# Layer 0's gate products from q and k: fp32 in four column strips instead of split fp32r one by one

## The chip, the cores and the metric
The kernel runs on one core of one Trainium2 chip, as one program. The metric is the device time of one execution in microseconds; the median of three runs of the kernel before is 917.6 us (916.42 to 917.76). The engines are named as the profile names them: PE is TensorE (PEld its weight loads), DVE is VectorE, ACT is ScalarE, POOL is GpSimd, SP is SyncE, whose queue issues most DMAs.

## What is computed
The reference is a trunk of two layers, an mLSTM mixer (layer 0) and a gated linear attention mixer (layer 1), for one sequence of 512 tokens and a model width of 1024. The part that the change touches is the gates of layer 0. Each of the 512 tokens gets eight gate values, two for each of four heads, from q, k and v, each 2048 wide:

```python
    q = jnp.einsum('bthd,hde->bthe', uch, _f32(wq))
    k = jnp.einsum('bthd,hde->bthe', uch, _f32(wk))
    v = jnp.einsum('bthd,hde->bthe', u.reshape(B, T, M_HEADS, M_HEAD_DIM), _f32(wv))
    gates = (jnp.einsum('bte,eg->btg', q.reshape(B, T, D_INNER), wg[:D_INNER])
             + jnp.einsum('bte,eg->btg', k.reshape(B, T, D_INNER), wg[D_INNER:2 * D_INNER])
             + jnp.einsum('bte,eg->btg', v.reshape(B, T, D_INNER), wg[2 * D_INNER:])
             + _f32(b_gate))
    log_i = gates[..., :M_HEADS]
    log_f = jax.nn.log_sigmoid(gates[..., M_HEADS:])
    hh = mlstm_chunked(q, k * (M_HEAD_DIM ** -0.5), v, log_i, log_f)
```

The gates go through running sums and maxima into exponentials, so they need nearly the full fp32 precision; q, k and v also feed the attention of each head.

## The kernel before
Activations lie with 128 channels on the partitions and the 512 tokens along the free axis, a `t2` tile of 128x512 (59 buffers of that kind). Nearly every product is made as three fp32r matmuls: an operand is split into a rounded part `hi` (an ACT cast) and the rest `lo` (a DVE subtraction), and hi*hi, hi*lo and lo*hi are added in PSUM. PSUM has eight banks, one 128x512 fp32 tile each.

The order of work is written out by hand as a list of jobs. `run_jobs` goes through it: before a job it loads and splits the weight chunks of the next jobs (three raw buffers, chunks split about three jobs ahead), then calls what `later(k, ...)` has put off to this job, then pops from `steps` and `spare`, then issues the job's own matmuls. Each engine runs its queue in the order in which this program issues it; SP's queue holds the loads of weights (`load_raw`, L155), of gate weights for v (L389) and the stores and loads of `uc_d` (L436, L712).

In layer 0, for each head: four `u` jobs (the input projection, then a convolution), two `v` jobs, and four q/k jobs (`qk_job`: two for q, then two for k). A q/k job makes two tiles of q or k with 24 matmuls and splits each into `qkh` and `qkl`. Two jobs later (three for head 0) `gate_add` multiplies each `qkh` and `qkl` with 16 columns of `wgr`, which hold the eight gate weights as `hi` and `lo` parts, into rows 0 to 15 of the bank `gacc`: four fp32r matmuls for a job, 16 jobs. The 64 matmuls and four more with the v part (`v_gates_end`) form one accumulation. The scores of a head (`score`) come after the second `u` job of the next head.

V of a head is copied from PSUM by ACT (`v_evac`), is then read by DVE and POOL for the v part of the gates (`v_gate`, popped from `spare` in later jobs), and stays in its four `t2` tiles until `split_v` of its head, after the gates are done (`decay`, `split_v`). After the last head come the `z` jobs, with `gates1` (copy of `gacc` to `gs`), `gates2` (two fp32 matmuls with the selection matrix `selg` add the hi and lo rows and spread them to 16 rows, then the row operations) and `gates3` between them.

Of the kernel before, what the change touches and what calls it, by code (L numbers as in the profile page):

```python
# [9 lines left out]
F32 = mybir.dt.float32  # L10
# [86 lines left out]
def tile_mlstm_gla(ctx, tc, xT, pvec, cst, wg, wgv, w_min, w_qk, w_v, w_mout,  # L97
# [11 lines left out]
    def t2(name, dt=F32):  # L109
        return tp.tile([P, T], dt, tag="t2", bufs=NT2, name=name)  # L110
# [10 lines left out]
    def mm(out, lhsT, rhs, start, stop, more=False):  # L121

        nc.tensor.matmul(out, lhsT=lhsT, rhs=rhs, start=start, stop=stop, skip_group_check=more)  # L123
# [13 lines left out]
    def split(hi, lo, src):  # L137
        nc.scalar.copy(hi, src)  # L138
        nc.vector.tensor_sub(lo, src, hi.bitcast(F32))  # L139
# [7 lines left out]
    def job(fn, *srcs, n=1, b=0, la=LA):  # L147
        jobs.append((fn, srcs, n, b, la))

    def later(k, fn):  # L150
        laters.append([k, fn])
# [214 lines left out]
    nc.vector.tensor_copy(csr[:, 3 * P:], cs[:, 4 * P:])  # L366

    wgs = t2("wgs")[:, 0:256].rearrange("p (a b) -> p a b", b=8)
    wgr = t2("wgr", F32R).rearrange("p (a b) -> p a b", b=16)
    nc.scalar.dma_start(wgs, wg)  # L370
    hhi, hlo = t2s("hhi", KD, F32R), t2s("hlo", KD, F32R)
    uc_d = dp.tile([KE, P, T], F32, name="uc_d")
    gacc = psum("gacc")
    gcount = [0]

    def gate_add(w, hi, lo):
        for r in (hi, lo):
            mm(gacc[0:16, :], w, r, gcount[0] == 0, False)
            gcount[0] += 1


    vg = cp.tile([P, NH, 4, 8], F32, name="vg")
# [18 lines left out]
    def v_gates(h):  # L401
        for g in (0, 1, 2, 3):
            v_gate_load(h, g)
        spare.extend([lambda g=g, i=i: v_gate(h, g, i) for g in range(8) for i in range(4)])
# [50 lines left out]
    def u_job(n):  # L455
        def run(chunk):
            ps = psum("u")
            if n < 4:
                proj(ps, chunk, ghi, glo)
                fps.append(ps)  # L460
            else:
                proj(ps, chunk, hhi, hlo)
                u_split(n, ps)
                u_conv(n, ps)
            if n == 2:
                acc = None
                for k in range(KD):
                    acc = add_square(acc, xt[k])
                st["accx"] = acc
                nc.scalar.copy(wgr[:, :, 0:8], wgs)  # L470
                nc.vector.tensor_sub(wgr[:, :, 8:16], wgs, wgr[:, :, 0:8].bitcast(F32))
            if n == 3:
                st["rsx"] = rstd_of([st["accx"]], D)
                u_scaled(range(4), fps)
                steps.extend([lambda k=k: h_step((k, k + 1)) for k in range(0, KD, 2)])

        job(run, ring(w_min[n]), b=3, la=1 if n == 2 else LA)

    def v_evac(h, pss):
        V[h] = t2s(f"V{h}", 4)  # L480
        for i in range(4):
            nc.scalar.activation(V[h][i], pss[i], AF.Copy, accum_out=vmean[:, 4 * h + i:4 * h + i + 1])  # L482
        c = vmean[:, 4 * h:4 * h + 4]
        nc.vector.tensor_scalar_mul(c, c, -1.0 / T)
        v_gates(h)

    def v_job(h, c):
        def run(chunk):
            if c == 0:
                st["v"] = [psum("v") for _ in range(4)]  # L490
            pss = st["v"]
            natural(pss, chunk, 2 * c, [uh[4 * h + i] for i in range(4)], [ul[4 * h + i] for i in range(4)], 4)
            if c == 1:
                later(1, lambda: v_evac(h, pss))

        job(run, ring(w_v[2 * h + c]), n=1, b=4)

    def qk_job(h, which, c):
        d = (q, kq)[which]

        def run(chunk):
            whi, wlo = chunk
            for e in range(2):
                n = 4 * h + 2 * c + e
                ps = psum("qk")
                for k in range(4):
                    wh, wl = part(whi, k * 256 + e * P, P), part(wlo, k * 256 + e * P, P)
                    mm(ps, wh, ch[4 * h + k], k == 0, False)
                    mm(ps, wh, cl[4 * h + k], False, False)
                    mm(ps, wl, ch[4 * h + k], False, k == 3)  # L510
                d[n] = t2("qkh", F32R), t2("qkl", F32R)
                split(*d[n], ps)

            def gates():
                for e in range(2):
                    n = 4 * h + 2 * c + e
                    gate_add(wgr[:, 16 * which + n, :], *d[n])

            later(2 if h else 3, gates)

        job(run, ring(w_qk[which, 2 * h + c]), n=1, b=(1, 4, 4, 6)[h])

    def score(h):
        A[h] = t5(f"A{h}")
        for sb in range(4):
            ps = psum("sc")
            ts = slice(sb * P, T)
            sl = slice(sb * P, (sb + 1) * P)
            o = ps[:, 0:WID[sb]]
            for i in range(4):  # L530
                n = 4 * h + i
                mm(o, kq[n][0][:, sl], q[n][0][:, ts], i == 0, False)
                mm(o, kq[n][0][:, sl], q[n][1][:, ts], False, False)
                mm(o, kq[n][1][:, sl], q[n][0][:, ts], False, i == 3)
            nc.scalar.mul(A[h][:, OFF[sb]:OFF[sb] + WID[sb]], o, float(T) ** -0.5)
# [52 lines left out]
    def rows(name):  # L588
        g[name] = t2(name)[0:R16, :]
        return g[name]  # L590

    def gates1():
        v_gates_end()
        nc.vector.memset(br.bitcast(F32), 0.0)
        nc.vector.memset(rows("zr"), 0.0)
        nc.scalar.copy(rows("gs"), gacc[0:16, :])

    def gates2():
        ips, fps = psum("ips"), psum("fps")
        mm(fps[0:R16, :], selg[0:16, 16:32], g["gs"], True, True)  # L600
        mm(ips[0:R16, :], selg[0:16, 0:16], g["gs"], True, True)
        gi, ab, lf = rows("gi"), rows("ab"), rows("lf")
        nc.scalar.activation(ab, fps[0:R16, :], AF.Abs, bias=col(PV_BF, R16))
        nc.vector.tensor_scalar(lf, fps[0:R16, :], scalar1=col(PV_BF, R16), scalar2=0.0,
                                op0=ALU.add, op1=ALU.min)
        use(LNEXP)
        nc.scalar.activation(ab, ab, AF.Exp, scale=-1.0)
        nc.scalar.activation(ab, ab, AF.Ln, bias=1.0)
        nc.scalar.activation(gi, ips[0:R16, :], AF.Identity, bias=col(PV_BI, R16))
        nc.vector.tensor_sub(lf, lf, ab)  # L610
        mrow, fm, gl, ar, bb = (rows(n) for n in ("mrow", "fm", "gl", "ar", "bb"))
        nc.vector.tensor_tensor(fm.rearrange("p (b t) -> p b t", t=P), lf.rearrange("p (b t) -> p b t", t=P),
                                selg[0:R16, 32:36].unsqueeze(2).broadcast_to([R16, 4, P]), op=ALU.mult)
        nc.vector.tensor_tensor_scan(gl, fm, g["zr"], 0.0, op0=ALU.add, op1=ALU.add)
        nc.vector.tensor_sub(ar, gi, gl)
        nc.vector.tensor_tensor_scan(mrow, lf, gi, 0.0, op0=ALU.add, op1=ALU.max)
        nc.vector.tensor_scalar_max(mrow, mrow, 0.0)
        nc.vector.tensor_sub(bb, gl, mrow)
# [15 lines left out]
    def split_scores(h):  # L634
        S[h] = t5("shi", F32R), t5("slo", F32R)
        split(*S[h], A[h])
# [20 lines left out]
    def weigh(h):  # L657
        nc.vector.tensor_mul(A[h], A[h], W[h])
# [86 lines left out]
            split(yhi[n], ylo[n], HC[h][vt])  # L745

    z_job(b=16)
    job(lambda: score(NH - 1))
    job(gates1)
    job(silu_z, n=0)  # L750
    z_job()
    job(silu_z, n=0)
    job(gates2)
    z_job()
    z_job()
# [2 lines left out]
    job(lambda: (decay(0), weigh(0), split_scores(0), split_v(0)))  # L758
    job(lambda: (load_uc(0), load_uc(1)), n=0)
    z_job()  # L760
    job(lambda: (decay(1), steps.extend([lambda: None, lambda: (weigh(1), split_scores(1))])))

    def head_steps(h):
        m_rstd(h)
        if h + 2 < NH:
            decay(h + 2)
        m_y(h, (0, 1))
        if h + 1 == NH:
            m_y(h, (2, 3))
            y_split(h, range(4))  # L770
        else:
            steps.extend([lambda: (split_v(h + 1), m_y(h, (2, 3)), silu_z(), load_uc(4 * h + 4), load_uc(4 * h + 5)),
                          lambda: None,
                          lambda: y_split(h, range(4))])
            if h + 2 < NH:
                steps.append(lambda: (weigh(h + 2), split_scores(h + 2)))
# [637 lines left out]
def _host(inputs):  # L1414
# [16 lines left out]
    for h in range(4):  # L1431
        for sb in range(4):
            j = 4 * h + sb
            for base in (0, 8):
                cst[base + h, 3 * P + j] = 1.0
                cst[base + 4 + h, 3 * P + 16 + j] = 1.0
            cst[j, 3 * P + 32:3 * P + 36] = (np.arange(4) >= sb)
            cst[j, 4 * P + j] = 1.0
            cst[32 + j, 4 * P + j] = 1.0
        cst[64 + 4 * h, 4 * P + 16 + h] = 1.0  # L1440
        cst[96 + 4 * h, 4 * P + 16 + h] = 1.0
# [49 lines left out]
```

## Time and profile before

| | |
|---|---|
| median of the runs | 917.6 us (916.42 to 917.76, 3 runs) |
| profiled execution | 917.5 us, of which the span of the instructions is 915.8 us |
| PE busy | 902.4 us (99%) |
| DVE busy | 630.6 us (69%) |
| ACT busy | 523.3 us (57%) |
| POOL busy | 183.2 us (20%) |
| DMA moved | 147.58 MB, mean 161 GB/s |

The busy time of an engine is the time in which at least one of its instructions was running. Matmuls overlap in their pipeline and their ends are modelled, so the distance between two starts says what one costs, not its duration. The granted clock is the share of TensorE's full clock. An idle engine costs nothing where another one sets the time.

### The profile page before, as it was taken

How to read it: one execution, taken by the hardware profiler on the slowest of the kernel's cores; microseconds unless marked ns; L12 is line 12 of the kernel's file. 1: busy time of each engine (PE TensorE's matmuls, PEld its weight loads, DVE VectorE, ACT ScalarE, POOL GpSimd, SP SyncE). 2: the span in 40 equal slices, each digit the busy share in tenths (PEclk: the TensorE clock that was granted, in tenths of full speed). 3: DMA queues.
4: the chain of work that ended last, by engine and by line, in shares of the span. 5: the costliest groups of instructions: out<-in, count | busy, mean ns of one | idle time of the engine just before them, and what ended most of it. 6: DMA issues, size and time to landing. Idle time of an engine off the chain costs nothing. (4 is left out here: it accounts for less than half of the span.)

```text
span 915.8 us, 12449 instructions
## 1 busy us (share of the span) xinstructions
PE 902.4 (99%) x4624; PEld 760.7 (83%) x4624; DVE 630.6 (69%) x916; ACT 523.3 (57%) x885; POOL 183.2 (20%) x162
## 2 busy tenths in 40 slices
PE   9999999999999999999999999999999999999995
PEld 6887878878877888899999997777888888888874
DVE  5999797886886668788658746743346547478854
ACT  6865685756654558866557626544435345365642
POOL 0022552262250043245002310421000000000121
PEclk9999999999999999999999999999999999999998
DMA  8334344352342223222775694995343736383776
GB/s 309 120 122 147 117 151 137 116 169 97 123 142 69 93 70 115 92 93 69 232 235 198 206 323 166 236 243 140 116 138 114 242 115 200 118 287 104 269 275 138
DMA packets 50882, 147.58 MB, mean 161 GB/s; under 512 B 5792, under 2 KB 10272, under 8 KB 50528
## 3 DMA queue, kind: packets, MB, share of 16 engines
q1 hardware_dynamic: 44832, 120.29, 39.7%
q0 software_dynamic: 5696, 26.22, 10.8%
q8 instruction: 38, 0.62, 0.3%
q14 instruction: 28, 0.23, 0.1%
q10 hardware_dynamic: 288, 0.22, 0.1%
HBM read 129.92 MB, written 34.60 MB: 180 GB/s over the span
## 5 line engine op out<-in xcount | busy, mean ns | idle before, releaser
L139 DVE TENSOR_TENSOR wlo<-raw,whi 128x1024 fp32r<-128x1024 f32 (+1 forms) x146 | 186.3, 1284 | 98.8 <-ACT whi L138 98.1
L138 ACT CAST whi<-raw 128x1024 fp32r<-128x1024 f32 (+1 forms) x146 | 149.9, 1036 | 79.0 <-PE gv L123 24.2
L394 POOL TENSOR_TENSOR vp<-V,wv 128x512 f32<-128x512 f32 x56 | 88.6, 1604 | 177.4 <-ACT V L482 92.6
L123 PE MATMUL op<-yhi,whi 128*128 128x256 f32 x256 | 73.5, 287 | 0.0
L123 PE MATMUL op<-yhi,wlo 128*128 128x256 f32 x256 | 72.5, 283 | 0.4 <-DVE wlo L139 0.4
L123 PE MATMUL op<-ylo,whi 128*128 128x256 f32 x256 | 72.8, 284 | 0.0
L397 DVE SCALAR_TENSOR_TENSOR vp<-V,wv 128x512 f32<-128x512 f32 x72 | 68.0, 987 | 0.0
L163 POOL DMA_DIRECT2D whi<-wpP x8 | 4.3, 536 | 244.7 <-DMA raw<-in_w_gout 216.9
L123 PE MATMUL gz<-g2h,whi 128*128 128x512 f32 x128 | 51.5, 403 | 0.5 <-PEq L1156 0.5
L123 PEld LDWEIGHTS op<-ylo,whi 128*128 128x128 f32 x256 | 49.1, 192 | 1.1 <-DVE ylo L139 0.6
L123 PE MATMUL gz<-g2h,wlo 128*128 128x512 f32 x128 | 49.9, 390 | 0.0
L123 PE MATMUL gz<-g2l,whi 128*128 128x512 f32 x128 | 49.8, 389 | 0.0
L123 PE MATMUL qk<-chi,whi 128*128 128x512 f32 x128 | 49.8, 389 | 0.0
L123 PE MATMUL qk<-chi,wlo 128*128 128x512 f32 x128 | 49.8, 389 | 0.0
L123 PE MATMUL qk<-clo,whi 128*128 128x512 f32 x128 | 49.8, 389 | 0.0
L123 PE MATMUL gv<-whi,g2h 128*128 128x512 f32 x128 | 49.8, 389 | 0.0
L123 PE MATMUL gv<-wlo,g2h 128*128 128x512 f32 x128 | 49.8, 389 | 0.0
L123 PE MATMUL gv<-whi,g2l 128*128 128x512 f32 x128 | 49.8, 389 | 0.0
L123 PEld LDWEIGHTS op<-yhi,wlo 128*128 128x128 f32 x256 | 49.1, 192 | 0.6 <-DVE wlo L139 0.6
L123 PEld LDWEIGHTS op<-yhi,whi 128*128 128x128 f32 x256 | 49.1, 192 | 0.5 <-issue 0.5
L123 PE MATMUL z<-hhi,whi 128*128 128x512 f32 x112 | 44.1, 394 | 0.0
L123 PE MATMUL z<-hlo,whi 128*128 128x512 f32 x112 | 43.7, 390 | 0.0
(286 smaller groups left out, 2503.9 us busy)
## 6 DMA issues: line engine op xcount, KB each, us to landing
raw<-in_w_min SPq DMA_DIRECT2D x30, 512.0 KB, 3.7
raw<-in_w_mout SPq DMA_DIRECT2D x29, 512.0 KB, 4.2
wv<-in_wgv SPq DMA_DIRECT2D x32, 256.0 KB, 3.6
raw<-in_w_qk SPq DMA_DIRECT2D x16, 512.0 KB, 3.7
raw<-in_w_gqk SPq DMA_DIRECT2D x16, 512.0 KB, 4.0
raw<-in_w_gz SPq DMA_DIRECT2D x16, 512.0 KB, 5.2
raw<-in_w_gv SPq DMA_DIRECT2D x16, 512.0 KB, 4.1
raw<-in_w_v SPq DMA_DIRECT2D x8, 512.0 KB, 3.5
```

Source lines behind the costliest of these rows:

```text
L123: nc.tensor.matmul(out, lhsT=lhsT, rhs=rhs, start=start, stop=stop, skip_group_check=more)
L138: nc.scalar.copy(hi, src)
L139: nc.vector.tensor_sub(lo, src, hi.bitcast(F32))
L163: nc.gpsimd.dma_start(to, of)
L394: nc.gpsimd.tensor_mul(j, V[h][i], w)
L397: nc.vector.scalar_tensor_tensor(j, V[h][i], 1.0, w, op0=ALU.mult, op1=ALU.mult, accum_out=o)
```

## The change
`gate_add` is called once for the four tiles of a head's q (and once for those of its k), after the second of the two jobs. It issues four fp32 matmuls, each with the eight unsplit gate weights of its tile from `wgs`, into rows 32i to 32i+7 of `gacc` at column position 32i of the array, so that each of the four has its own strip of 32 columns. For this every q and k tile is also copied from PSUM to a `t2` tile `q32` by ACT, ahead of the split. `wgr` is gone. `gates1` copies four groups of eight rows instead of 16 rows into `gs`, which is a whole tile now and is zeroed on POOL by `gates0`; `selg` has four blocks of rows instead of two, and the two matmuls of `gates2` take all 128 rows. To make room, V of heads 0 to 2 is stored to DRAM (`v_d`) after its copy from PSUM, and loaded into new `t2` tiles by `load_v` before it is split. The DMAs of both directions are on SP's queue.

```diff
-    wgr = t2("wgr", F32R).rearrange("p (a b) -> p a b", b=16)
...
-    def gate_add(w, hi, lo):
-        for r in (hi, lo):
-            mm(gacc[0:16, :], w, r, gcount[0] == 0, False)
-            gcount[0] += 1
+    def gate_add(parts):
+
+        for i, (w, r) in enumerate(parts):
+            nc.tensor.matmul(gacc[32 * i:32 * i + 8, :], lhsT=w, rhs=r, start=gcount[0] == 0,
+                             stop=i > 0 and gcount[0] == 7, tile_position=(0, 32 * i))
+        gcount[0] += 1
...
-                nc.scalar.copy(wgr[:, :, 0:8], wgs)
-                nc.vector.tensor_sub(wgr[:, :, 8:16], wgs, wgr[:, :, 0:8].bitcast(F32))
...
+    v_d = dp.tile([4 * NH - 4, P, T], F32, name="v_d")
+
+    def load_v(h):
+
+        if h < NH - 1:
+            V[h] = t2s(f"Vr{h}", 4)
+            for i in range(4):
+                nc.sync.dma_start(V[h][i], v_d[4 * h + i])
...
         nc.vector.tensor_scalar_mul(c, c, -1.0 / T)
+        if h < NH - 1:
+            for i in range(4):
+                nc.sync.dma_start(v_d[4 * h + i], V[h][i])
         v_gates(h)
...
                 d[n] = t2("qkh", F32R), t2("qkl", F32R)
+                q32[n] = t2("q32")
+                nc.scalar.copy(q32[n], ps)
                 split(*d[n], ps)
 
-            def gates():
-                for e in range(2):
-                    n = 4 * h + 2 * c + e
-                    gate_add(wgr[:, 16 * which + n, :], *d[n])
-
-            later(2 if h else 3, gates)
+            if c:
+                parts = [(wgs[:, 16 * which + n, :], q32.pop(n)) for n in range(4 * h, 4 * h + 4)]
+                later(2 if h else 3, lambda: gate_add(parts))
...
+    def gates0():
+        g["gs"] = t2("gs")
+        nc.gpsimd.memset(g["gs"], 0.0)
+
...
-        nc.scalar.copy(rows("gs"), gacc[0:16, :])
+        for i in range(4):
+            r = slice(32 * i, 32 * i + 8)
+            if i % 2:
+                nc.vector.tensor_copy(g["gs"][r, :], gacc[r, :])
+            else:
+                nc.scalar.copy(g["gs"][r, :], gacc[r, :])
...
-        mm(fps[0:R16, :], selg[0:16, 16:32], g["gs"], True, True)
-        mm(ips[0:R16, :], selg[0:16, 0:16], g["gs"], True, True)
+        mm(fps[0:R16, :], selg[:, 16:32], g["gs"], True, True)
+        mm(ips[0:R16, :], selg[:, 0:16], g["gs"], True, True)
...
-    job(lambda: score(NH - 1))
+    job(lambda: (gates0(), score(NH - 1)))
...
+    job(lambda: load_v(0), n=0)
     job(gates2)
...
+    job(lambda: load_v(1), n=0)
     job(lambda: (decay(1), steps.extend([lambda: None, lambda: (weigh(1), split_scores(1))])))
...
         if h + 2 < NH:
+            load_v(h + 2)
             decay(h + 2)
...
-            for base in (0, 8):
+            for base in (0, 32, 64, 96):
```

## Rows read from the trace of the kernel before

**Rows 1.** The page, busy us (share of the span) and instructions of each engine
```profile
PE 902.4 (99%) x4624; PEld 760.7 (83%) x4624; DVE 630.6 (69%) x916; ACT 523.3 (57%) x885; POOL 183.2 (20%) x162
```

**Rows 2.** The page, 40 slices of the span: busy tenths and granted clock
```profile
PE   9999999999999999999999999999999999999995
...
PEclk9999999999999999999999999999999999999998
```

**Rows 3.** Waits of PE's weight loads, 40 to 430 us: us in total, times, longest
```profile
PEld z L123 <- issue: 1.1, 2, 0.9
...
PEld gacc L123 <- DVE qkl L139: 0.7, 2, 0.4
```

**Rows 4.** The tile `gacc`: count, duration min/median/max in ns, first and last start
```profile
L123 PE MATMUL gacc<-qkh,wgr x32: 388/397/398, 67.9 to 279.6; 128*16 128x512 f32 x32
...
L123 PE MATMUL gacc<-qkl,wgr x32: 393/396/403, 68.2 to 279.9; 128*16 128x512 f32 x32
```

**Rows 5.** Timeline of PE around one gate group: start us, us, engine, line, operation
```profile
193.95 0.39 PE L123 MATMUL qk<-chi,wlo 128*128 128x512 f32 x1
194.18 0.40 PE L123 MATMUL gacc<-qkh,wgr 128*16 128x512 f32 x1
...
194.88 0.39 PE L123 MATMUL gacc<-qkl,wgr 128*16 128x512 f32 x1
195.11 0.40 PE L123 MATMUL qk<-chi,whi 128*128 128x512 f32 x1
195.35 0.39 PE L123 MATMUL qk<-clo,whi 128*128 128x512 f32 x1
```

**Rows 6.** Timeline of PE around the two fp32 products of `gates2`
```profile
294.07 0.39 PE L123 MATMUL z<-hhi,wlo 128*128 128x512 f32 x1
294.38 1.03 PE L123 MATMUL fps<-gs,cs 16*16 16x512 f32 x2
295.25 1.02 PE L123 MATMUL ips<-gs,cs 16*16 16x512 f32 x2
296.20 0.50 PE L123 MATMUL z<-hhi,whi 128*128 128x512 f32 x1
296.54 0.39 PE L123 MATMUL z<-hlo,whi 128*128 128x512 f32 x1
```

**Rows 7.** Timeline of PE around the v part of the gates
```profile
287.43 0.28 PE L123 MATMUL sc<-qkl,qkh 128*128 128x128 f32 x1
287.55 0.28 PE L123 MATMUL sc<-qkh,qkl 128*128 128x128 f32 x1
287.75 1.04 PE L123 MATMUL gacc<-cs,vg 128*8 128x128 f32 x8
288.72 0.50 PE L123 MATMUL z<-hhi,whi 128*128 128x512 f32 x1
289.06 0.40 PE L123 MATMUL z<-hlo,whi 128*128 128x512 f32 x1
```

**Rows 8.** ACT by line, 51 to 290 us: busy us, mean ns of one, idle before
```profile
L138 ACT CAST qkh<-qk 128x512 fp32r<-128x512 f32 x32 | 18.2, 591 | 28.3 <-PE qk L123 22.3 <-DVE vp L397 6.0
...
L554 ACT COPY z<-z 128x512 f32<-128x512 f32 x1 | 0.6, 587 | 4.2 <-DVE vp L397 4.2
```

**Rows 9.** Stretches of layer 0's heads: busy us and instructions, clock, DMA share, GB/s
```profile
core 0: us, PE busy (x) PEld busy (x) DVE busy (x) ACT busy (x) POOL busy (x), PEclk, DMA share, GB/s
51.60:290.00 238.40, 238.40 (x1111) 193.85 (x1110) 196.17 (x299) 145.43 (x300) 88.59 (x56) 1.00 0.40 128
62.50:78.50 16.00, 16.00 (x72) 12.33 (x71) 15.93 (x22) 10.78 (x18) 5.43 (x4) 1.00 0.26 91
```

**Rows 10.** Timelines: two weight splits on DVE and the jobs on PE
```profile
68.53 1.21 DVE L139 TENSOR_TENSOR wlo<-raw,whi 128x1024 fp32r<-128x1024 f32 x1
...
75.29 0.39 PE L123 MATMUL u<-hhi,whi 128*128 128x512 f32 x1
...
291.95 1.23 DVE L139 TENSOR_TENSOR wlo<-raw,whi 128x1024 fp32r<-128x1024 f32 x1 [5.25 <-ACT whi L138]
...
307.65 0.50 PE L123 MATMUL z<-hhi,whi 128*128 128x512 f32 x1
```

**Rows 11.** SP's queue, 40 to 430 us: waits, and `uc_d` and `ucr`'s issues, landing
```profile
SPq L155 <- DVE wlo L139: 259.5, 54, 12.6
...
SPq L712 <- PE num L123: 9.5, 3, 7.7
...
L436 SPq DMA_DIRECT2D uc_d<-us x16: 326/327/423, 43.5 to 249.3; - x16
...
uc_d<-us SPq DMA_DIRECT2D x16, 256.0 KB, 3.7
ucr<-uc_d SPq DMA_DIRECT2D x16, 256.0 KB, 3.9
```

**Rows 12.** Timeline of ACT, 287.7 to 297 us
```profile
288.83 0.58 ACT L596 COPY gs<-gacc 16x512 f32<-16x512 f32 x1 [0.69 <-PE gacc L123]
```

More of the change, by code (lines that the diff above doesn't have):

```diff
@@ L496, in v_job @@
         job(run, ring(w_v[2 * h + c]), n=1, b=4)
+    q32 = {}
     def qk_job(h, which, c):
```

## The prediction

> **What bounds the kernel now.** I read the page's busy times first: PE is busy 902.4 us of a span of 915.8, DVE 630.6, ACT 523.3 [rows 1]. The slices say the same along the run: PE stands at 9 in every slice but the last and its granted clock at 9 in all but the last too [rows 2], so it runs on the higher of its two levels, 2.4 GHz, and no stage has a gap to fill. The list of what PE's weight loads waited for has, in all of layer 0's stretch from 40 to 430 us, nothing over 1.1 us; the gate products of the change appear there with 0.7 us, behind the subtraction that makes `qkl` [rows 3]. PE's queue therefore sets the time: a microsecond of PE taken out of layer 0 or put into it moves everything behind it by a microsecond, as long as ACT, DVE and the DMAs go on covering it. The chain that ended last is of no use for this, since it only follows the tail.
>
> **What is removed.** The gate products of q and k are 64 matmuls with 16 stationary columns and 512 moving ones, 32 on `qkh` and 32 on `qkl` [rows 4], in 16 groups of four, one for each q/k job. A group runs from 194.18 to 195.11 us: four steps of 0.23, 0.93 us in all, and the neighbours on both sides keep their own step of 0.23 [rows 5]. 16 x 0.93 = 14.9 us of PE go. The small split of `wg` into `wgr` (one ACT cast, one DVE subtraction) goes too; neither is on PE's path, so I book nothing.
>
> **What PE gets instead.** Eight groups of four fp32 products (8 stationary columns, 512 moving). The trace has fp32 products of 512 moving columns: `fps` and `ips` in `gates2` [rows 6]. Each shows as two instructions (x2 for one call), and `ips` starts 0.87 us after `fps`: one product is two passes of 0.435 us, one after the other. A pass is thus nearly twice the step of 0.23 of an fp32r product of the same width [rows 5], and a product nearly four. So one by one the new products would be 32 x 0.87 = 27.8 us, more than the 14.9 removed; all hangs on how much the four column strips overlap, and no row of this trace shows two strips at work together. The bounds for a group are: all four side by side, two passes, 0.87 us; no overlap, eight passes, 3.48 us.
>
> Between them I choose by the order of the queue. The rows of `fps` and `ips` show that the two passes of one product stand next to each other, and that each begins when the one ahead has streamed [rows 6]; throughout the rows PE's matmuls start in the order of the program [rows 5 to 7]. The two passes of one product use the same strip, so the second must wait for the first. If starts keep the queue's order, the first pass of product 2 can't start before the second pass of product 1, though its strip is free. Then the passes pair up as 1a, 1b+2a, 2b+3a, 3b+4a, 4b: five steps, 5 x 0.435 = 2.18 us.
>
> The Trainium skill, "TensorE: Matmul & The Clock Gate", Part 3, "The mechanism", states that matmuls start and end strictly in queue order and only weight loads are pulled ahead. By that rule the five steps hold, and it speaks against this change; the trace agrees as far as its starts go, and shows no two strips at once.
>
> Then there are the edges. Where the array goes from full-width fp32r products to fp32 ones in a narrow strip and back, time is lost: from 287.55 to 289.06 us there are 1.51 us, of which one `sc` step is 0.11, eight passes of 128 columns (a quarter of 0.435 each) 0.87 and one `z` step 0.23, so 0.30 is left over [rows 7]. Around `fps` and `ips`, 294.07 to 296.54 is 2.47, less the steps themselves, 0.23 + 4 x 0.435 + 0.23 = 2.20: 0.27 [rows 6]. The old gate groups, also narrow but fp32r, lose nothing (195.35 - 193.95 = 1.40 for six steps of 0.23) [rows 5]. The bounds of the edge are 0 and 0.30; I take 0.30, since rows 7 have the new groups' form (8 columns, fp32, the same accumulator).
>
> Sum for PE: 8 x (2.18 + 0.30) = 19.8 us added, 14.9 removed: **4.9 us more**. With edges of nothing it would be 8 x 2.18 = 17.4, 2.5 us more.
>
> **What ACT gets.** 32 copies of a 128x512 product from PSUM into `q32`, ahead of the `qkh` cast. The nearest rows are the `z` copy, 0.587 us, and the cast, 0.591 [rows 8]: 32 x 0.59 = 18.9 us. In the stretch of the four heads, 51.6 to 290 us, ACT is busy 145.4 of 238.4 us and DVE 196.2 [rows 9]; ACT rises to 164, still under. The delay matters by order: `qkl` waits for `qkh`, which comes 0.59 us later for each product, and DVE runs its queue in order. Tightest is head 0, where DVE is busy 15.93 of 16 us between 62.5 and 78.5 [rows 9]. What hides it is the lead of the weight splits: the `wlo` that ends at 69.74 is the one that the `u` job starting at 75.29 needs, 5.6 us later [rows 10]. Head 0's eight copies are 4.7 us, so the lead covers them by about 1 us. I book 0, and a gain is excluded, since work is only added; if that cover is gone, the price is what exceeds it. The gates themselves no longer wait for `qkl`, only for the copy, which gives back up to the 0.7 us of rows 3; I leave it out, as the pitch of the groups hardly shows it.
>
> **What moves to DRAM.** 12 stores and 12 loads of 256 KB on SP's queue. An issue there takes 0.33 us and lands after about 3.7 to 3.9, as `uc_d` and `ucr` show [rows 11]. A store waits for ACT's `V`, and behind it in SP's queue stand the gate-weight and the weight loads. Those weight loads wait for DVE's `wlo` of a later split anyway (259.5 us of waits), and ACT does that split's cast after `V`; the store's wait lies inside theirs. The loads of V take `t2` buffers and may wait for one: `load_uc`, in the same place, waited at most 7.7 us [rows 11]. Weight chunks there are split far ahead of their use: the `wlo` from 291.95 to 293.18 us is that of the `z` job right after `gates3`, which starts at 307.7, 14.5 us later [rows 10]. The DMA engines are at 0.40 in that stretch [rows 9]; 6.3 MB more is small beside it. Cost 0, bound 2 us; a gain is excluded, since no wait of PE's list is for a buffer [rows 3].
>
> **The end of the gates.** One ACT copy of 0.58 us becomes two on ACT and two on DVE, and a POOL memset joins. `gs` is done at 289.4 and first needed at 294.38 [rows 6, 12]; some 1.5 us more is covered by the `z` job between. 0.
>
> **Sum.** The profiled run took 917.5 us (span 915.8, 1.7 around it); the median of the runs is 917.6. 917.5 + 4.9 = **922.4 us**.
>
> **The rivals.**
> *Full overlap.* If each strip has its own queue, 1a to 4a run together and then 1b to 4b: 8 x (0.87 + 0.30) = 9.4 us, 5.5 less than removed, **912.0**; with no edges 8 x 0.87 = 7.0, 909.6. For it: the strips share neither weights nor output partitions. Against it: the passes' order in the queue. It decides when a group takes fewer than (14.9/8 - 0.30)/0.435 = 3.6 steps. The same page of the Trainium skill, "Measured speedup vs the span model", gives a pack of tiles one matmul's duration plus about 4 ns a tile; read with both passes as one matmul, it is this rival. No run here shows it yet.
> *In between.* Four steps (a second pass that hides once): 8 x (1.74 + 0.30) = 16.3, 1.4 more, 918.9, no change that can be told.
> *It doesn't do what it says.* If fp32 passes of different strips don't overlap, 8 x (3.48 + 0.30) = 30.2 us, 15.3 more, **932.8**. For it: every fp32 pair seen is serial; against: all those share a strip.
> *The copies or V's loads come out on PE.* Five steps hold and PE also waits where head 0's lead is used up, or for a load behind a blocked SP queue: another 2 to 4 us, 924.4 to 926.4.
>
> **How the numbers follow.** Five steps 0.52, full overlap 0.26, in between 0.07, no overlap 0.09, five steps with waits 0.06. Under 0.2% (1.8 us) this kernel's measurement can't tell from no change: its three runs span 916.42 to 917.76. Slower 0.52 + 0.09 + 0.06 = 0.67, same 0.07, faster 0.26. The likeliest case alone reaches from 920.0 (no edges) to 923.2 (0.1 us more in each group). The range takes in full overlap without edges, 909.5, and the waits, 927; only the serial case, 0.09, is left out.
>
> **What would show it.** In the changed trace a gate group is eight matmul rows: by my forecast the starts come as single, pair, pair, pair, single with 0.435 between, and some 2.5 us pass from the last full-width product's end to the next; rival one shows all within 0.9 us, the serial one eight steps. The waits should show no PE row behind `q32`, `wlo` or `raw`. The forecast is wrong if second passes start after later products' first passes, or if PE waits in head 0.

## The result

The changed kernel took 911.64 us (911.44 to 912.22, four runs) against 917.44 for the kernel before: a ratio of 0.994, with an interval of 0.9922 to 0.9957. It is 5.8 us faster; 922.4 was forecast, with 909.5 to 927 as the range. The time fell into the range, but by the case that had 0.26, the full overlap, priced at 912.0.

The page of the changed kernel, first busy us of each engine, then the slices of PE and of its granted clock:

```profile
PE 896.8 (99%) x4624; PEld 756.1 (83%) x4624; DVE 628.8 (69%) x917; ACT 539.2 (59%) x917; POOL 182.7 (20%) x163
...
PE   9999999999999999999999999999999999999995
...
PEclk9999999999999999999999999999999999999998
```

PE is still busy 99% of a span that went from 915.8 to 910.0 us, at the same clock, so the reading that PE sets the time held [rows 1, 2]. PE's busy time itself fell by 5.6 us, from 902.4 to 896.8. ACT has 32 instructions more and 15.9 us more to do. The 5.8 us are to be sought in PE's queue, and there the gate groups are what differs. The timeline of PE around one of the eight groups (start us, us, engine, line, operation), and under it the tile `gacc` in the stretch from 131.7 to 132.1 us and in that from 132.5 to 132.7:

```profile
131.45 0.39 PE L123 MATMUL qk<-chi,wlo 128*128 128x512 f32 x1
131.77 1.04 PE L378 MATMUL gacc<-q,wgs 128*8 128x512 f32 x8
132.75 0.50 PE L123 MATMUL qk<-chi,whi 128*128 128x512 f32 x1
133.08 0.39 PE L123 MATMUL qk<-clo,whi 128*128 128x512 f32 x1
```

```profile
L378 PE MATMUL gacc<-q,wgs x4: 596/596/597, 131.8 to 131.8; 128*8 128x512 f32 x4
...
L378 PE MATMUL gacc<-q,wgs x4: 592/592/592, 132.2 to 132.2; 128*8 128x512 f32 x4
```

All eight passes run in 1.04 us: four start at 131.8 and four at 132.2. So there are two steps, not five. From 131.45 to 133.08 there are 1.63 us; less the neighbours' two steps of 0.23 that is 1.17 for a group, 0.87 for two passes and 0.30 of edge. All eight groups have this length in the trace. Together they take 9.4 us where the sixteen old ones took 14.9 [rows 5]: 5.5 us less, which is nearly all of the 5.8. The 0.3 that is left can't be told from what varies ahead of the change: the first `ssq` product starts at 28.98 us in the profiled execution before and at 28.29 in this one, and at 29.36 in another profiled execution of this same kernel.

What the change moves elsewhere stays off PE's path. ACT's copies and casts by line, 50 to 284 us (busy us, mean ns, idle before), then the stretch of the heads and that of head 0's q/k jobs (busy us and instructions of each engine, clock, DMA share, GB/s):

```profile
L138 ACT CAST qkh<-qk 128x512 fp32r<-128x512 f32 x32 | 19.5, 610 | 1.0 <-DVE vp L398 1.0
L526 ACT COPY q<-qk 128x512 f32<-128x512 f32 x32 | 19.2, 600 | 14.6 <-PE qk L123 14.6
```

```profile
50.90:283.70 232.80, 232.80 (x1110) 188.14 (x1109) 193.45 (x300) 160.33 (x330) 86.73 (x57) 1.00 0.46 149
61.00:77.00 16.00, 16.00 (x75) 12.31 (x74) 15.10 (x20) 12.43 (x23) 6.74 (x5) 1.00 0.37 119
```

The copies cost ACT 19.2 us (18.9 was worked out), and take the place of idle time that ACT had in front of `qkh`: 28.3 us before [rows 8], 14.6 plus 1.0 now. ACT rises to 160 us in the heads, DVE stays about where it was, and the stretch itself is 5.6 us shorter, 232.80 in place of 238.40 [rows 9]. In the waits of PE's weight loads, 40 to 430 us, there is no entry for V's loads:

```profile
PEld qk L123 <- issue: 2.6, 3, 0.9
PEld gacc L378 <- issue: 2.1, 6, 0.4
PEld u L123 <- issue: 1.7, 2, 0.9
PEld sc L123 <- issue: 1.7, 2, 0.9
...
PEld u L123 <- DVE qkl L139: 0.9, 1, 0.9
...
PEld gacc L378 <- DVE qkl L139: 0.4, 1, 0.4
PEld gacc L378 <- ACT whi L138: 0.4, 1, 0.4
```

These rows look like stalls and are the groups themselves. The 0.9 stands eight times (3 + 2 + 2 + 1), once behind each group, on whatever product comes next, and the 0.4 eight times (6 + 1 + 1), once ahead of each. That is weight loading at rest around and during the eight passes. The names behind the arrows are only what happened to end last.

### The profile page after: what moved, and what is told of

It is laid out like the page before. It is cut to its first block, busy times and chain, and to the rows that moved or that the text cites. A ratio compares the mean times of both kernels' runs of the same rounds, so it can differ in the third digit from the quotient of the medians.

```text
span 910.0 us, 12523 instructions
## 1 busy us (share of the span) xinstructions
PE 896.8 (99%) x4624; PEld 756.1 (83%) x4624; DVE 628.8 (69%) x917; ACT 539.2 (59%) x917; POOL 182.7 (20%) x163
## 5 line engine op out<-in xcount | busy, mean ns | idle before, releaser
L395 POOL TENSOR_TENSOR vp<-V,wv 128x512 f32<-128x512 f32 x56 | 86.2, 1560 | 173.4 <-ACT V L490 72.0
```

The source lines that it names most:

```text
L395: nc.gpsimd.tensor_mul(j, V[h][i], w)
```

## The experiments

Theory after the result: a strip runs on its own. A pass waits for the passes of its own strip alone, and a pass for a free strip starts ahead of others that stand before it in the queue. The rival is the step on record, that starts keep the queue's order; then the gain would have to come from something else in the change.

**One strip in place of four.**

```diff
-            nc.tensor.matmul(gacc[32 * i:32 * i + 8, :], lhsT=w, rhs=r, start=gcount[0] == 0,
-                             stop=i > 0 and gcount[0] == 7, tile_position=(0, 32 * i))
+            nc.tensor.matmul(gacc[0:8, :], lhsT=w, rhs=r, start=gcount[0] == 0 and i == 0,
+                             stop=False, tile_position=(0, 0))
```

> The changed kernel with the four fp32 products of a group in one column strip (position 0, the same eight rows of the accumulator) in place of four; the rest stays. If the side-by-side strips are what made the change faster, a group goes from two steps to eight: 8 x (8 x 0.435 + 0.30) = 30.2 us in place of 9.4, 20.9 us more than the changed kernel's 911.6: 932.5. If the gain came from what else the change does (no wait for qkl, V out of the buffers), the time stays near 912 to 918.

It took 932.0 us (ratio 1.0156, interval 1.0137 to 1.0175). A group in PE's timeline:

```profile
136.84 0.39 PE L123 MATMUL qk<-chi,wlo 128*128 128x512 f32 x1
137.16 3.60 PE L378 MATMUL gacc<-q,wgs 128*8 128x512 f32 x8
140.69 0.50 PE L123 MATMUL qk<-chi,whi 128*128 128x512 f32 x1
141.03 0.40 PE L123 MATMUL qk<-clo,whi 128*128 128x512 f32 x1
```

From 136.84 to 141.03 there are 4.19 us. Less the neighbours' two steps, 0.46, the same eight passes in one strip take 3.73 us with their edge, 2.56 more than in four strips: 8 x 2.56 = 20.5 us. PE's busy time rose by 19.9, from 896.8 to 916.7, and the time by 20.4 from 911.64, or by 19.3 from the 912.74 that the changed kernel took when it was run again (below). So fp32 in one strip would have lost 14.5 us against the kernel before (932.0 to 917.55). The strips made the whole gain.

**Two strips, in block order.**

```diff
-            nc.tensor.matmul(gacc[32 * i:32 * i + 8, :], lhsT=w, rhs=r, start=gcount[0] == 0,
-                             stop=i > 0 and gcount[0] == 7, tile_position=(0, 32 * i))
+            j = i // 2
+            nc.tensor.matmul(gacc[32 * j:32 * j + 8, :], lhsT=w, rhs=r, start=gcount[0] == 0 and i % 2 == 0,
+                             stop=i == 3 and gcount[0] == 7, tile_position=(0, 32 * j))
...
-                q32[n] = t2("q32")
+                q32[n] = t2("q" + "abcd"[n % 4])
```

> The changed kernel with two strips: of the four products a, b, c, d in the queue's order, a and b go to strip 0, c and d to strip 1; their copies are named qa to qd so that the trace tells them apart. If a strip runs on its own and only passes of the same strip wait for each other, c starts with a, ahead of b, and a group takes four steps: 8 x (4 x 0.435 + 0.30) = 16.3 us in place of 9.4, 918.5. If starts keep the queue's order, c waits for b's second pass to start and a group takes seven steps: 8 x (7 x 0.435 + 0.30) = 26.8, 929.0.

It took 918.71 us (ratio 1.0012, interval 1.0003 to 1.0022). Here the names show the order. The code issues `qa`, `qb`, `qc`, `qd`; PE's timeline has:

```profile
73.26 0.60 PE L379 MATMUL gacc<-qa,wgs 128*8 128x512 f32 x1
73.27 0.60 PE L379 MATMUL gacc<-qc,wgs 128*8 128x512 f32 x1
73.69 0.59 PE L379 MATMUL gacc<-qa,wgs 128*8 128x512 f32 x1
73.70 0.59 PE L379 MATMUL gacc<-qc,wgs 128*8 128x512 f32 x1
74.12 0.59 PE L379 MATMUL gacc<-qb,wgs 128*8 128x512 f32 x1
74.14 0.59 PE L379 MATMUL gacc<-qd,wgs 128*8 128x512 f32 x1
74.55 0.59 PE L379 MATMUL gacc<-qb,wgs 128*8 128x512 f32 x1
74.56 0.59 PE L379 MATMUL gacc<-qd,wgs 128*8 128x512 f32 x1
```

`qc` starts 0.01 us after `qa`, and 0.85 us ahead of `qb`, which is issued before it. Both passes of `qc` overtake both of `qb`. In the program that is built from this kernel, PE's queue holds the passes as `qa`, `qa`, `qb`, `qb`, `qc`, `qc`, `qd`, `qd`, so the order was not changed before the chip. Four steps, as the theory says, and 918.5 was expected. The rival's seven steps and 929.0 are out: starts don't keep the queue's order across strips.

The Trainium skill, "TensorE: Matmul & The Clock Gate", Part 3, "The mechanism", has it that matmuls are never reordered, in start or end. These rows differ, and the measurement decides: in strips of their own, later matmuls start first.

**How far ahead.**

```diff
-            if c:
-                parts = [(wgs[:, 16 * which + n, :], q32.pop(n)) for n in range(4 * h, 4 * h + 4)]
+            if c and which:
+                parts = [(wgs[:, 16 * w + n, :], q32.pop((w, n))) for w in range(2) for n in range(4 * h, 4 * h + 4)]
...
+            j = n // 4
+            nc.tensor.matmul(gacc[32 * j:32 * j + 8, :], lhsT=w, rhs=r, start=gcount[0] == 0 and i == 0,
+                             stop=gcount[0] == 3 and n == 7, tile_position=(0, 32 * j))
```

> The changed kernel with the q and k products of a head in one call and two strips in block order: the four q products (qa to qd) all go to strip 0, then the four k products (ka to kd) to strip 1, so that the first pass of ka stands behind seven passes of strip 0. If a strip's passes start whenever their strip is free, however deep, ka starts with qa and a call takes eight steps: 4 x (8 x 0.435 + 0.30) = 15.1 us in place of 9.4, 917.3. If only a few passes are looked past, ka starts some steps later, 0.435 us a step for each of four calls. If starts keep the queue's order, 15 steps: 27.3 us, 929.5.

It took 923.77 us (ratio 1.0069, interval 1.0051 to 1.0088), the middle case. The code issues `qa` to `qd` for strip 0, then `ka` to `kd` for strip 1:

```profile
83.72 1.03 PE L380 MATMUL gacc<-qa,wgs 128*8 128x512 f32 x2
84.58 1.02 PE L380 MATMUL gacc<-qb,wgs 128*8 128x512 f32 x2
85.44 0.59 PE L380 MATMUL gacc<-qc,wgs 128*8 128x512 f32 x1
85.45 0.60 PE L380 MATMUL gacc<-ka,wgs 128*8 128x512 f32 x1
85.87 0.59 PE L380 MATMUL gacc<-qc,wgs 128*8 128x512 f32 x1
85.88 0.59 PE L380 MATMUL gacc<-ka,wgs 128*8 128x512 f32 x1
...
87.17 1.02 PE L380 MATMUL gacc<-kc,wgs 128*8 128x512 f32 x2
88.03 1.02 PE L380 MATMUL gacc<-kd,wgs 128*8 128x512 f32 x2
```

Strip 1 stands empty for four steps, until `qc` has started; then `ka` goes, past three waiting passes (the second of `qc`, both of `qd`). With more than three waiting it did not go, and all four calls of the trace show this. In the run before, `qc` also went past three (the second of `qa`, both of `qb`). The call takes 12 steps: 4 x (12 x 0.435 + 0.30) = 22.1 us, 12.7 more than the changed kernel, so 924.3; 923.77 was measured. The change's own order needs three as well: the first pass of its fourth product stands behind the second passes of the first three.

**The old gates with the new traffic.**

```diff
-    def gate_add(parts):
-
-        for i, (w, r) in enumerate(parts):
...
+    def gate_add(w, hi, lo):
+        for r in (hi, lo):
+            mm(gacc[0:16, :], w, r, gcount[0] == 0, False)
+            gcount[0] += 1
```

> The gate products as before the change (64 fp32r matmuls, 16 columns), with the changed kernel's 32 copies to q32 (read by nobody) and V's trip to DRAM. If both are hidden, 917.4 as before, within 0.5. If the copies or the trip cost PE time, 919 or more, with waits of PE behind whi, wlo or chi in the four heads. If V's absence from the buffers or the end of some wait made part of the gain, under 916.5.

It took 917.26 us beside 917.55 for the kernel before: ratio 0.9997, interval 0.9988 to 1.0006. The 32 copies, 12 stores and 12 loads cost nothing that can be measured and bring nothing. The stretches of the heads and of head 0's q/k jobs show where they went:

```profile
51.20:289.60 238.40, 238.40 (x1111) 193.91 (x1110) 193.98 (x299) 161.00 (x332) 88.36 (x56) 1.00 0.44 142
62.10:78.10 16.00, 16.00 (x72) 12.44 (x71) 15.95 (x21) 13.22 (x25) 6.22 (x4) 1.00 0.37 129
```

ACT has 161 us instead of 145, and between 62 and 78 us DVE stays full at 15.95 of 16 while PE works on without a gap. That fits the forecast's reading that the lead of the splits takes the delay; no run varied that lead.

**V stays.**

```diff
-        if h < NH - 1:
-            for i in range(4):
-                nc.sync.dma_start(v_d[4 * h + i], V[h][i])
...
-        if h < NH - 1:
-            V[h] = t2s(f"Vr{h}", 4)
-            for i in range(4):
-                nc.sync.dma_start(V[h][i], v_d[4 * h + i])
+        pass
```

> The changed kernel without V's trip: V of heads 0 to 2 stays in its t2 tiles, no stores, no loads. If the trip is hidden and the buffers still suffice, 911.6 as the changed kernel. If V's room is needed, loads or splits wait for buffers and PE waits behind them: 913 or more. If the trip itself cost time, under 911.

It took 912.5 us, ratio 0.9947 (0.9933 to 0.9961); the changed kernel had 0.994 (0.9922 to 0.9957) and, run again, 0.9951 (0.9938 to 0.9965). 912.5 lies between the forecast's cases of 911.6 and of 913 or more, and so does the changed kernel's second measurement, 912.74. The intervals lie on each other, and PE's busy time is 896.9 us beside 896.8. So the 59 buffers hold the copies even with V in place, and the trip brings or costs nothing that can be told from the noise.

**q and k in one call.** The eight products of a head go two to a strip, `gate_add` is called four times.

```diff
+        for n, (w, r) in enumerate(parts):
+            i = n % 4
+            nc.tensor.matmul(gacc[32 * i:32 * i + 8, :], lhsT=w, rhs=r, start=gcount[0] == 0 and n < 4,
+                             stop=i > 0 and gcount[0] == 3 and n > 3, tile_position=(0, 32 * i))
```

> The changed kernel with the q and the k products of a head in one call: eight products, two a strip, four calls in place of eight. If strips run on their own and the 0.30 us of edge is paid once a call, 4 x (4 x 0.435 + 0.30) = 8.2 us in place of 9.4: 910.4. If starts keep the queue's order within the longer call (product 5 goes to strip 0 again), the second four still follow in the same way, and what differs is the edge alone. If the edge belongs to each set of four, 911.6 as now; if the longer life of the copies runs out of buffers, later than 911.6.

It took 911.4 us, with single runs from 910.34 to 912.77; that spread is larger than the 1.2 us that were looked for, so the time alone doesn't decide. PE's timeline around one of the four calls does:

```profile
84.19 0.39 PE L123 MATMUL u<-hhi,wlo 128*128 128x512 f32 x1
84.50 1.90 PE L379 MATMUL gacc<-q,wgs 128*8 128x512 f32 x16
86.34 0.50 PE L123 MATMUL sc<-qkh 128*128 128x512 f32 x1
86.67 0.40 PE L123 MATMUL sc<-qkl,qkh 128*128 128x512 f32 x1
```

From 84.19 to 86.67 there are 2.48 us. Less 0.46 for the neighbours that is 2.02 for a call: four steps, 1.74, and about one edge, 0.28. Two groups of the changed kernel take 2 x 1.17 = 2.34, so each head saves 0.3 us, some 1.3 us in all; PE's busy time went from 896.8 to 895.3. The edge is paid once a call.

**More in strips.** The v part of the gates and the two selection products of `gates2`.

```diff
-            mm(gacc[0:8, i * P:(i + 1) * P], vg[:, 0, i, :], ident, False, i == 3)
+            nc.tensor.matmul(gacc[32 * i:32 * i + 8, i * P:(i + 1) * P], lhsT=vg[:, 0, i, :], rhs=ident, start=False,
+                             stop=True, tile_position=(0, 32 * i))
...
+        ips = ips[32:32 + R16, :]
         mm(fps[0:R16, :], selg[:, 16:32], g["gs"], True, True)
-        mm(ips[0:R16, :], selg[:, 0:16], g["gs"], True, True)
+        nc.tensor.matmul(ips, lhsT=selg[:, 0:16], rhs=g["gs"], start=True, stop=True, tile_position=(0, 32))
```

> The changed kernel with two more places in strips: the four products of the v part each in its own strip (two steps of 0.11 in place of eight), and the two selection products of gates2 side by side (two steps of 0.435 in place of four). If strips run on their own there too, 0.65 + 0.87 = 1.5 us less: 910.1, if PE still sets the time at those places. If what follows the gates waits for other engines instead, 911.6.

It took 909.81 us (ratio 0.992, interval 0.9906 to 0.9933); 910.1 was expected. The v part as it was [rows 7] and now:

```profile
281.81 0.28 PE L123 MATMUL sc<-qkh,qkl 128*128 128x128 f32 x1
282.02 0.40 PE L411 MATMUL gacc<-cs,vg 128*8 128x128 f32 x8
282.35 0.50 PE L123 MATMUL z<-hhi,whi 128*128 128x512 f32 x1
```

The eight passes span 0.40 us in place of 1.04. From the last `sc` product's start to the first `z` product's there are 0.54 us in place of 1.17 [rows 7], 0.63 less. That is the six steps of 0.11 that went, so the edge stays.

**All of it.** Both of the last two, with the last head's call put off to stand right ahead of the v part (`later(2 if 0 < h < NH - 1 else 3, ...)`). The changed kernel ran beside it.

> The two places of the run before that gained (v part and selection in strips), with q and k of a head in one call, and the last head's call put off to stand right ahead of the v part. Strips on their own: 1.5 us from the two places, 4 x 0.30 = 1.2 us from four edges fewer, 0.3 us from one edge shared by the last call and the v part: 3.0 us less than the changed kernel, 0.9967 of its time. If PE no longer sets the time in the heads, or an edge is paid at each change of the kind of product rather than of the strip width, 1.5 us or less.

> The changed kernel itself once more, on the same chip as the run of all strips, so that the two can be set side by side: 5.6 to 6.0 us less than the kernel before.

All strips took 909.59 us (ratio to the kernel before 0.9911, interval 0.9897 to 0.9925), the changed kernel on the same chip 912.74 (0.9951). That is 3.15 us less, where 3.0 were expected. Single runs of the two kernels spread over 2.3 and 1.6 us, so the tenths mean little; PE's busy time fell by 3.3, from 896.8 to 893.5. An edge is paid for each visit to the narrow strips, not for each set of products. The last call and the v part share theirs, and `fps` and `ips` start together:

```profile
278.56 0.28 PE L123 MATMUL sc<-qkh,qkl 128*128 128x128 f32 x1
278.76 1.90 PE L379 MATMUL gacc<-q,wgs 128*8 128x512 f32 x16
280.48 0.40 PE L412 MATMUL gacc<-cs,vg 128*8 128x128 f32 x8
280.82 0.50 PE L123 MATMUL z<-hhi,whi 128*128 128x512 f32 x1
281.15 0.39 PE L123 MATMUL z<-hlo,whi 128*128 128x512 f32 x1
...
286.49 0.60 PE L123 MATMUL fps<-gs,cs 128*16 128x512 f32 x1
286.49 0.60 PE L625 MATMUL ips<-gs,cs 128*16 128x512 f32 x1
```

From 278.56 to 281.15 there are 2.59 us. Four steps of 0.435, two of 0.11, and the neighbours' 0.11 and 0.23 make 2.30, so 0.29 is left: one edge for both.

It isn't fp32 by itself that costs the edge. The kernel before has fp32 products over the full width (`ssq`, 128 columns) among fp32r ones:

```profile
28.75 0.39 PE L123 MATMUL u<-ghi,wlo 128*128 128x512 f32 x1
28.98 1.02 PE L123 MATMUL ssq<-sq,cs 128*128 128x512 f32 x2
29.43 0.79 PE L123 MATMUL z<-ghi,whi 128*128 128x512 f32 x1
30.06 0.40 PE L123 MATMUL z<-glo,whi 128*128 128x512 f32 x1
```

From 28.75 to 30.06 there are 1.31 us, and the steps alone make 0.23 + 2 x 0.435 + 0.23 = 1.33: no edge. The old gate products, 16 columns and fp32r, had none either [rows 5]; why not, no run shows.

Run again, the changed kernel missed its own forecast: 912.74 us is 4.6 less than the kernel before beside it (917.3), where 5.6 to 6.0 were expected. By its interval it is 3.2 to 5.7 us less, by that of the first measurement 3.9 to 7.2, so the two agree within their noise, and PE's busy time is 896.8 us in both profiles. About 1 us between measurements of one kernel is what all comparisons of medians above have to allow for.

By its ratio the run with all strips is the fastest of the study, but its interval overlaps that of the run with only the two more places in strips (0.9906 to 0.9933). No run has fp32r products in strips.

## Why the prediction was wrong

- **PE sets the time**: right. Each run's time followed PE's queue. Against the first measurement of the changed kernel, the rise was 20.4 us for 20.5 worked out (one strip), 7.1 for 6.9 (two strips) and 12.1 for 12.7 (deep block); against its second it is 1.1 us smaller each time. PE's busy time, which doesn't count the wait at the start, rose by 19.9, 6.8 and 12.0.
- **What is removed**, 14.9 us: right [rows 5].
- **One product is two passes of 0.435 us**: right; the passes start 0.43 apart in every run, and in one strip eight of them follow each other.
- **The overlap of the strips**: wrong, and this is the step that failed. The forecast took five steps because "starts keep the queue's order". The rows it rested on [rows 5 to 7] have no two products in strips of their own, so order and strip can't be told apart; they show that a pass waits for its own strip, and I read from them that it waits for the queue. The run with two strips separates the two: `qc` starts 0.85 us ahead of `qb`. That step mis-sized the group, 2.18 us of passes where 0.87 was measured; 8 x 1.31 = 10.5 us of the 10.8 from 922.4 to 911.64.
- **The edge**, 0.30 us a group: right, taken from the v part, which had the same form.
- **The copies, V's trip, the end of the gates**, booked at 0: right. The old gates with all the new traffic took 0.9997 of the kernel before. The four copies of `gates1` run one after the other between ACT and DVE, from 282.61 to 285.25 us, 2.6 us where one copy took 0.58 [rows 12]; `fps` starts at 288.11, still behind them.
- **The rivals**: full overlap was priced right, 912.0 against 911.64. Its break-even of 3.6 steps is borne out from both sides: two steps (911.64) are faster than before, and four steps (918.71, priced at 918.9) are not: 1.0012 (1.0003 to 1.0022). Against it I had set the order of the queue, which falls here.

## What to carry to other kernels

Products with few output rows are worth placing in strips of the array of their own: the time of a group is the number of passes in its fullest strip plus one edge, so put as many narrow products as there are into one visit, and issue them round the strips rather than strip by strip: in blocks of four products a strip four steps were lost, in blocks of two none. A resource that no row of a trace shows at work leaves both ends open; rows that share one strip say nothing about two. Work added to engines with idle time in the same stretch (19 us on ACT, 6 MB of DMA) cost nothing that could be measured here.

## What the runs showed of the hardware

- fp32 passes in different column strips start about 0.01 us apart (73.26 and 73.27) and run side by side; a pass waits for its own strip and not for passes ahead of it in others, as far as the next point allows.
- A pass for a free strip went past three waiting passes of another strip, in two runs, and did not go while more were waiting (strip 1 empty from 83.72 to 85.45 us). Whether three is a fixed depth was not varied further.
- A visit to narrow fp32 strips costs about 0.30 us at its edges, alike for eight passes in four strips (1.17 = 0.87 + 0.30) and in one strip (3.73 = 3.43 + 0.30); also with sixteen passes in one call (2.02 = 1.74 + 0.28). Full-width fp32 products (`ssq`) had none, nor had the old 16-column fp32r products at position 0 [rows 5].
- The same kernel's start varies by about a microsecond: the first `ssq` product begins at 28.29 us in one profiled execution of the changed kernel and at 29.36 in another. Spans of single executions are better compared from a mark behind the start, or by PE's busy time where PE sets the time.
